# Attention probabilities of a query tile in one tile of up to 16 key tiles instead of two of 8, with a ring of five instead of ten

## The chip, the cores and the metric

One core of one Trainium2 chip runs the kernel. The metric is device time in microseconds (us). The engines named below are TensorE (PE; its weight loads are PEld), VectorE (DVE), ScalarE (ACT), GpSimd (POOL) and the DMA queue of SyncE (SP).

## What is computed

The reference is one layer of a decoder trunk on 2048 tokens of width 1024: a mixer of four groups and a gated feed-forward part. The change touches the two attention groups, FoX and NSA. Cut to what matters, per head and query row:

```
s = q @ k.T * scale + bias          # FoX: decay c_q - c_k, causal
p = softmax(where(mask, s, -1e30))  # NSA: table bias; masks of selected blocks / a window of 512
o = p @ v
```

FoX has 4 heads with all earlier keys. NSA has 4 heads with three branches: compressed keys, the selected blocks, and a sliding window. A query tile is 128 rows, so there are 16 query tiles. A query tile `qt` has up to `qt + 1` key tiles of 128 in FoX and in the selected branch, and at most 5 in the window branch.

## The kernel before

The attention stage works in units: one branch, one head and a pair `p` of query tiles (`q0 = 2p`, `a` = 0 or 1 for the tile of the pair). `fox_units` makes 4 x 8 units; `nsa_units` makes, per head, the pairs 0 to 3 of the selected branch and the pairs 0 to 7 of the window branch, and after all four heads the pairs 4 to 7 of the selected branch. The text calls these stretches FoX, early NSA (48 units) and late NSA (16 units). The blocks of the compressed branch (`add_cmp`) run beside FoX.

A unit goes through these steps (`add_unit`, lines as in the profile):

- score: two matmuls per group of up to 4 key tiles into an `S` bank of PSUM (L1045, L1046). `S` has two banks.
- bias: a DVE operation adds the bias to `S`, writes the sum into the tile `P` and keeps the row minimum in `mn` (L1060).
- expo: ACT takes the exponential of `P` in place and sums each row (L1082); an instruction that reads the sum out (ACTIVATION_READ_ACCUMULATOR) belongs to it. It runs only after the last bias of the row, since it needs the final minimum.
- turn: PE transposes two key tiles of both query tiles into a `tp` bank (L1118). Such a group of two key tiles is a slot.
- split: ACT, DVE and POOL make the high and low parts `ph` and `pl` of `tp` in one of three ways (L908, L911, L916, L920, L925). Way 0 is ACT and DVE, way 1 ACT, DVE and POOL, way 2 ACT twice and POOL.
- pv: PE multiplies both parts with the values into `obank` (L1140). At the end of a unit `obank` is copied by ACT (L962), transposed (L967), scaled into `t` on DVE (L975) or on ACT (L973), and added by POOL.

`P` is a tile of 128 x 1024, eight key tiles, and its ring holds `PBUFS = 10`. A row of more than eight key tiles takes two of them, `P[a][0]` and `P[a][1]`, has two expos and a `sums` operation on POOL (L1097) that adds the two row sums. A tile is taken by the bias that writes its first part and comes free with the last turn that reads it.

The order on all engines is written by a planner (`Plan.run`). Each operation has a key, and of those that can start at about the same time the smallest key is taken. The scores of a unit have the key of the slot 11 ahead of its first turn (`LEAD`), the expos of 2 ahead (`ELEAD`). The way of a split, and whether `t` is on ACT or on DVE, are chosen by the planner from what is queued on the two engines (`best`). On the chip each engine runs its own list in this order; an instruction that waits holds all behind it on its engine.

Of the kernel before, what the change touches and what calls it, by code (L numbers as in the profile page):

```python
# [12 lines left out]
F32 = mybir.dt.float32  # L13
# [24 lines left out]
R_FQ, R_FK, R_NQ, R_KC, R_KSW, R_POS = 46, 47, 48, 49, 50, 51  # L38
NROW = 83
LEAD = 11  # L40
PBUFS = 10
NPH = 6
NPF = 3
NS = 2
# [128 lines left out]
def kernel(ctx, tc, x, norm_mix, w_in, lru_conv_w, lru_conv_b, lru_w_gates, lru_b_gates,  # L173
# [4 lines left out]
    PE, ACT, DVE, POOL, SP = nc.tensor, nc.scalar, nc.vector, nc.gpsimd, nc.sync  # L178
# [16 lines left out]
    ident = const.tile([128, 128], F32, name="ident")  # L195
# [586 lines left out]
    with ExitStack() as B:  # L782
# [6 lines left out]
        pp = B.enter_context(tc.tile_pool(name="pp", bufs=PBUFS, reuse_waits="tile"))  # L789
# [15 lines left out]
        def buf(name):  # L805
            return Buf(rings[name])
# [192 lines left out]
        def add_unit(u, s0):  # L999
# [4 lines left out]
            c = {}  # L1004
            P, exps = [{}, {}], [{}, {}]
            order, pads, summed = [], [], []
            for a in range(2):
                qt = q0 + a
                w = qt + 1 - los[a]
                pad = -w % 4 if u["sel"] else 0  # L1010
                pads.append(pad)
                if u["near"] and w == 5:
                    parts = [(0, 3), (3, 2)]
                else:
                    cuts = sorted({0, w} | set(range(4 - pad, w, 4)))
                    parts = [(p, x - p) for p, x in zip(cuts, cuts[1:])]
                order += [(n, a, p, pw, w) for n, (p, pw) in enumerate(parts)]
                for x in range(0, w + pad, 8):
                    P[a][x // 8] = buf("P")
                if u["sel"] and qt >= 8:  # L1020
                    def both(a=a, qt=qt):
                        c["bt", a] = sm.tile([128, 512], F32, name="bt", tag="bt", bufs=3)
                        POOL.tensor_add(c["bt", a].rearrange("p (b k) -> p b k", k=64),
                                        win[:, h, 128:640].rearrange("p (b k) -> p b k", k=64),
                                        selm[:, qt - 8, 2 * qt - 6:2 * qt + 2, None].to_broadcast([128, 8, 64]))
                    bb = buf("bt")
                    prev["bt"] = [add("Pool", 1.23, lead - 1, both, take=[bb],
                                      after=[tabop, selop[qt]] + prev["bt"])]
                    summed.append((bb, prev["bt"][0]))
            lastT = [None, None]  # L1030
            for n, a, p, pw, w in sorted(order):
                pa = p + pads[a]
                qt, lo = q0 + a, los[a]
                b0 = lo + p
                m = 2 if pw == 1 else pw
                more = [(max(t0, b0), min(t1, b0 + pw), fn) for t0, t1, fn in u["extra"](qt)]
                more = [x for x in more if x[0] < x[1]]
                Sb = buf("S")

                def score(a=a, qt=qt, b0=b0, pw=pw, m=m, more=more, n=n):  # L1040
                    S = c["S", a, n] = pss.tile([128, 512], F32, name="S", tag="S")
                    qs = slice((qt % 4) * 128, (qt % 4) * 128 + 128)
                    ks = u["k"].tile[:, b0 * 128:(b0 + m) * 128]
                    dst = S[:, :m * 128]
                    PE.matmul(dst, u["q"].tile[:, 0, qs], ks, start=True, stop=False)  # L1045
                    PE.matmul(dst, u["q"].tile[:, 1, qs], ks, start=False, stop=True)  # L1046
                    for t0, t1, fn in more:
                        PE.matmul(S[:, (t0 - b0) * 128:(t1 - b0) * 128], identr, fn(t0, t1), start=False, stop=True,
                                  skip_group_check=True)

                opens = n == 0 or pa % 8 == 0
                selects = u["sel"] and qt >= 8 and p + pw == w

                def bias(a=a, qt=qt, b0=b0, pw=pw, pa=pa, n=n, opens=opens, selects=selects):
                    if n == 0:
                        c["mn", a] = sm.tile([128, 4], F32, name="mn", tag="mn")
                    if opens:
                        c["P", a, pa // 8] = pp.tile([128, 1024], F32, name="P", tag="P")
                    x0, mn = pa % 8 * 128, c["mn", a]
                    DVE.tensor_tensor_reduce(c["P", a, pa // 8][:, x0:x0 + pw * 128], c["S", a, n][:, :pw * 128],  # L1060
                                             c["bt", a] if selects else u["bias"](qt, b0, b0 + pw), 1.0,
                                             mn[:, n - 1:n] if n else big, OP.add, OP.min, mn[:, n:n + 1])
                S = add("PE", 0.107 * (max(m, 2) + len(more)), lead + n * 0.01, score, take=[Sb],
                        use=[u["k"].buf, u["q"].buf],
                        after=[u["k"].op, u["q"].op] + prev["S"])
                prev["S"] = [S]
                Pb = P[a][pa // 8]
                cb, cops = u["biases"](qt, b0)
                if selects:
                    cb, cops = [summed[a][0]], [summed[a][1]]  # L1070
                lastT[a] = add("DVE", dve_time(pw * 128), lead + n * 0.01, bias, take=[Pb] if opens else [],
                               use=[Sb] + cb + ([] if opens else [Pb]),
                               after=[S] + cops + ([lastT[a]] if n else []))
                if p + pw == w:
                    for x in P[a]:
                        c0, c1 = pads[a] * 128 if x == 0 else 0, min(8, w + pads[a] - 8 * x) * 128

                        def expo(a=a, x=x, c0=c0, c1=c1, n=n):
                            if "sum" not in c:
                                c["sum"] = sm.tile([128, 2, 2], F32, name="sum", tag="sum")  # L1080
                            t = c["P", a, x][:, c0:c1]
                            ACT.activation(t, t, AF.Exp, bias=c["mn", a][:, n:n + 1], scale=-1.0,  # L1082
                                           accum_out=c["sum"][:, x, a:a + 1])
                        exps[a][x] = add("Activation", exp_time(c1 - c0), s0 - ELEAD + 0.1 * x, expo, use=[P[a][x]],
                                         after=[lastT[a]])
# [23 lines left out]
            for gi, g in enumerate(groups):  # L1109
# [5 lines left out]
                def turn(cells=cells, tp=tp):  # L1115
                    tp["tp"] = pst.tile([128, 2, 256], F32, name="tp", tag="tp")
                    for si, a, kt in cells:
                        PE.transpose(tp["tp"][:, si, a * 128:(a + 1) * 128],  # L1118
                                     c["P", a, kt // 8][:, kt % 8 * 128:(kt % 8 + 1) * 128], ident)
                used = sorted({(a, kt // 8) for _, a, kt in cells})  # L1120
                runs = []
                for si, sl in enumerate(g):
                    if sl[0] == sl[1]:
# [446 lines left out]
    with ExitStack() as Dx:  # L1570
# [156 lines left out]
        x = dict(x0)  # L1727
# [211 lines left out]
```

## Time and profile before

| | |
|---|---|
| median of 3 runs | 2710.84 us (2707.81 to 2711.39) |
| the profiled execution | 2708.36 us, of which span 2706.6 us |
| PE busy over the span | 2618.8 us (97%) |
| attention stage, 590 to 1196 us of the span | 606 us |

The stage lies in three stretches: FoX from 590 to about 850 us, early NSA to about 1040 us and late NSA to 1196 us. Feed-forward work follows it and needs its results, so idle time of PE in the stage is time of the whole. "Busy" counts an engine's instructions as the profiler shows them; the ends of matmuls are modelled.

### The profile page before, as it was taken

Reading aid. Unit: us, or ns where it says so; the run is one execution under the profiler, and the core shown is the slowest. Engines: PE = TensorE matmul, PEld = TensorE weight load, DVE = VectorE, ACT = ScalarE, POOL = GpSimd, SP = SyncE. Lnnn points to the kernel's source line nnn. Section 1 sums busy time; section 2 is a strip of 40 time slices with the busy share of each in tenths; the row PEclk is TensorE's granted clock in tenths of the full one; section 3 lists DMA queues with packets and bytes.
Section 4 is the critical chain, followed back from the end, with each engine's and each line's share of the span. In section 5 each row is a group of like instructions: output and inputs, shape, how many; then the busy total and the mean of one; then the engine's idle time right before and its main releaser. Section 6 shows DMA issues by size and latency. Waiting matters only on the chain.

```text
span 2706.6 us, 39620 instructions
## 1 busy us (share of the span) xinstructions
PE 2618.8 (97%) x13483; PEld 2207.1 (82%) x13483; DVE 1720.9 (64%) x3757; ACT 1339.4 (49%) x2916; POOL 976.2 (36%) x1103
## 2 busy tenths in 40 slices
PE   7999988999988999999999999999999999999999
PEld 5799767888987998888877888887888888888887
DVE  5763487347899889877777566667666555333333
ACT  5432475149988898885544333334233324333331
POOL 1101124214576577750234433433441123224440
PEclk9999999999999999999999999999999999999999
DMA  5444313264332211047855544455543235664653
GB/s 167 118 113 117 119 59 131 76 176 112 101 88 62 65 48 40 24 157 229 256 191 164 186 137 159 157 163 155 176 158 107 79 112 183 215 192 127 185 183 101
DMA packets 314808, 364.73 MB, mean 135 GB/s; under 512 B 25503, under 2 KB 214126, under 8 KB 313838
## 3 DMA queue, kind: packets, MB, share of 16 engines
q1 hardware_dynamic: 312430, 358.02, 42.5%
q10 hardware_dynamic: 2176, 4.19, 0.4%
q8 instruction: 106, 1.74, 0.3%
q14 instruction: 96, 0.79, 0.1%
HBM read 240.24 MB, written 121.90 MB: 134 GB/s over the span
## 4 chain that ended last, share of the span: by engine, by line
PE 77%; DVE 9%; issue 6%; DMA 3%; ACT 3%; POOL 2%; SPq 0%; POOLq 0%; DVEq 0%; ACTq 0%
PE gu L1758 9%; PE gu L1757 9%; PE gu L1756 9%; PE d L1885 5%; PE d L1887 5%; PE d L1886 5%; PE obank L1140 5%; PE tp L1118 4%; PE z L216 4%; PE z L217 4%; PE z L215 4%; PE S L1045 3%; PE S L1046 2%; PE px L215 2%; PE px L217 2%
## 5 line engine op out<-in xcount | busy, mean ns | idle before, releaser
L1756 PE MATMUL gu<-xh,g 128*128 128x512 f32 x1232 | 487.6, 396 | 7.6 <-DVE gq L1718 4.8
L1757 PE MATMUL gu<-xh,g 128*128 128x512 f32 x1232 | 487.0, 395 | 2.1 <-POOL g L1543 2.1
L1758 PE MATMUL gu<-xl,g 128*128 128x512 f32 x1232 | 486.7, 395 | 1.7 <-DVE xl L1666 1.7
L1543 POOL TENSOR_TENSOR g<-guraw,g 128x512 fp32r<-128x512 f32 x136 | 185.6, 1385 | 520.8 <-ACT g L1542 510.4
L1816 DVE TENSOR_TENSOR a<-araw,a 128x512 fp32r<-128x512 f32 x150 | 117.1, 783 | 268.9 <-ACT a L1815 268.9
L1756 PEld LDWEIGHTS gu<-xh,g 128*128 128x128 f32 x1232 | 232.4, 189 | 63.2 <-issue 5.6
L1757 PEld LDWEIGHTS gu<-xh,g 128*128 128x128 f32 x1232 | 232.4, 189 | 56.8 <-POOL g L1543 3.1
L1758 PEld LDWEIGHTS gu<-xl,g 128*128 128x128 f32 x1232 | 232.3, 189 | 56.7 <-DVE xl L1666 2.6
L925 POOL TENSOR_TENSOR pl<-pf,ph 128x512 fp32r<-128x512 f32 x174 | 224.0, 1294 | 109.1 <-ACT ph L911 47.8
L1082 ACT ACTIVATE P<-P,mn 128x1024 f32<-128x1024 f32 (+7 forms) x256 | 226.4, 892 | 17.7 <-DVE mn L1060 17.3
L1815 ACT CAST a<-araw 128x512 fp32r<-128x512 f32 x150 | 93.2, 622 | 279.2 <-PE d L1887 262.7
L1885 PE MATMUL d<-b,a 128*128 128x512 f32 x584 | 231.0, 396 | 0.0
L1886 PE MATMUL d<-b,a 128*128 128x512 f32 x584 | 231.0, 396 | 0.0
L1887 PE MATMUL d<-b,a 128*128 128x512 f32 x584 | 231.0, 396 | 0.0
L1140 PE MATMUL obank<-ph,v 128*128 128x256 f32 (+1 forms) x744 | 198.6, 294 | 3.7 <-ACT ob L962 3.6
L1118 PE MATMUL tp<-ident,P 128*128 128x128 f32 x1368 | 199.5, 273 | 2.0 <-DVE t L975 0.9
L1045 PE MATMUL S<-k,q 128*128 128x512 f32 (+2 forms) x432 | 175.5, 409 | 15.8 <-DVE mn L1060 11.0
L1140 PE MATMUL obank<-pl,v 128*128 128x256 f32 (+1 forms) x744 | 185.3, 283 | 3.4 <-POOL pl L925 1.9
L1118 PEld LDWEIGHTS tp<-ident,P 128*128 128x128 f32 x1368 | 160.1, 141 | 15.3 <-DVE t L975 1.2
L1827 POOL TENSOR_TENSOR b<-braw,b 128x512 fp32r<-128x512 f32 x73 | 101.9, 1409 | 182.7 <-ACT b L1826 181.2
L1046 PE MATMUL S<-k,q 128*128 128x512 f32 (+2 forms) x432 | 152.6, 355 | 0.0
L1542 ACT CAST g<-guraw 128x512 fp32r<-128x512 f32 x228 | 130.0, 618 | 42.5 <-DVE guraw L1613 34.9
(512 smaller groups left out, 6256.3 us busy)
## 6 DMA issues: line engine op xcount, KB each, us to landing
guraw<-in_w_gate_up_dram SPq DMA_DIRECT2D x88, 512.0 KB
araw<-hf_d SPq DMA_DIRECT2D x150, 256.0 KB
hf_d<-uq SPq DMA_DIRECT2D x88, 256.0 KB
q<-qk_d SPq DMA_DIRECT2D x80, 256.0 KB
hf_d<-gq SPq DMA_DIRECT2D x66, 256.0 KB
xt<-in_x_dram SPq DMA_DIRECT2D x32, 512.0 KB
xraw<-xf_d SPq DMA_DIRECT2D x24, 512.0 KB
dnraw<-in_w_down_dram SPq DMA_DIRECT2D x44, 256.0 KB
```

The lines of the kernel that those rows point to most:

```text
L925: POOL.tensor_sub(tp["pl"], tp["pf"], f(tp["ph"]))
L1045: PE.matmul(dst, u["q"].tile[:, 0, qs], ks, start=True, stop=False)
L1046: PE.matmul(dst, u["q"].tile[:, 1, qs], ks, start=False, stop=True)
L1082: ACT.activation(t, t, AF.Exp, bias=c["mn", a][:, n:n + 1], scale=-1.0, accum_out=c["sum"][:, x, a:a + 1])
L1118: PE.transpose(tp["tp"][:, si, a * 128:(a + 1) * 128], c["P", a, kt // 8][:, kt % 8 * 128:(kt % 8 + 1) * 128], ident)
L1140: PE.matmul(c["o"][:, cs], u["v"].tile[:, kt, :], tp[x][:, si, cs], start=gi == 0 and i == 0, stop=last and i == len(todo) - 1, skip_group ...
L1756: PE.matmul(p, wh[:, k], xh[:, k], start=j < 4 and k == 0, stop=False, skip_group_check=True)
L1757: PE.matmul(p, wl[:, k], xh[:, k], start=False, stop=False, skip_group_check=True)
L1758: PE.matmul(p, wh[:, k], xl[:, k], start=False, stop=k == HK - 1, skip_group_check=True)
L1885: PE.matmul(p, a[0][:, ts], w[0], start=first, stop=False, skip_group_check=True)
L1886: PE.matmul(p, a[0][:, ts], w[1], start=False, stop=False, skip_group_check=True)
L1887: PE.matmul(p, a[1][:, ts], w[0], start=False, stop=stop_, skip_group_check=True)
```

## The change

`PBUFS` goes from 10 to 5 and a new constant `WIDTH = 16` takes the place of every 8 in the division of a row into tiles. `P` becomes 128 x 2048, so that every row has one tile, one expo and no `sums`. The ring takes the same 40 KiB of each partition. A row of 8 key tiles or less, which took one of ten tiles, takes one of five.

```diff
-PBUFS = 10
+PBUFS = 5
+WIDTH = 16
...
-                for x in range(0, w + pad, 8):
-                    P[a][x // 8] = buf("P")
+                for x in range(0, w + pad, WIDTH):
+                    P[a][x // WIDTH] = buf("P")
...
-                opens = n == 0 or pa % 8 == 0
+                opens = n == 0 or pa % WIDTH == 0
...
-                        c["P", a, pa // 8] = pp.tile([128, 1024], F32, name="P", tag="P")
-                    x0, mn = pa % 8 * 128, c["mn", a]
+                        c["P", a, pa // WIDTH] = pp.tile([128, WIDTH * 128], F32, name="P", tag="P")
+                    x0, mn = pa % WIDTH * 128, c["mn", a]
...
-                        c0, c1 = pads[a] * 128 if x == 0 else 0, min(8, w + pads[a] - 8 * x) * 128
+                        c0, c1 = pads[a] * 128 if x == 0 else 0, min(WIDTH, w + pads[a] - WIDTH * x) * 128
...
-                                     c["P", a, kt // 8][:, kt % 8 * 128:(kt % 8 + 1) * 128], ident)
-                used = sorted({(a, kt // 8) for _, a, kt in cells})
+                                     c["P", a, kt // WIDTH][:, kt % WIDTH * 128:(kt % WIDTH + 1) * 128], ident)
+                used = sorted({(a, kt // WIDTH) for _, a, kt in cells})
```

The planner writes a new order on all engines. One line is added ahead, so a line of the changed kernel has a number one higher.

ACT in early NSA, at the window branch of head 2, pair 5. Before, the two exponentials are the first row, and the last row copies the unit's first slot:

```order
L1082 ACTIVATE P,sum<-P,mn 128x640 x2
L908 COPY pf<-tp 128x512
L1082 ACTIVATE P,sum<-P,mn 128x640
L962 COPY ob<-obank 128x256
L908 COPY pf<-tp 128x512
L911 CAST ph<-tp 128x512
L908 CAST ph<-tp 128x256
L908 CAST ph<-tp 128x512
L908 COPY pf<-tp 128x512
L1082 ACTIVATE P,sum<-P,mn 128x640
L908 CAST ph<-tp 128x256
L908 COPY pf<-tp 128x512
```

Now the two exponentials are the first and the third row, and the last row casts the unit's first slots:

```order
L1083 ACTIVATE P,sum<-P,mn 128x640
L974 ACTIVATE t<-fp,r 128x128 x2
L1083 ACTIVATE P,sum<-P,mn 128x640
L909 COPY pf<-tp 128x512
L909 CAST ph<-tp 128x512
L1083 ACTIVATE P,sum<-P,mn 128x640
L963 COPY ob<-obank 128x256
L909 CAST ph<-tp 128x256
L909 CAST ph<-tp 128x512 x2
```

Between the unit's second exponential and the first use of its transposed tile lie 5 instructions instead of 10.

ACT in late NSA, at the selected branch of head 1, pair 7, with rows of 15 and 16 key tiles. Before, each row has two exponentials, and the last row here casts the first slot:

```order
L1082 ACTIVATE P,sum<-P,mn 128x896
L908 COPY pf<-tp 128x512
L911 CAST ph<-tp 128x512
L908 CAST ph<-tp 128x512 x3
L1082 ACTIVATE P,sum<-P,mn 128x1024
L908 COPY pf<-tp 128x512
L911 CAST ph<-tp 128x512
L1082 ACTIVATE P,sum<-P,mn 128x1024 x2
L908 CAST ph<-tp 128x256
L908 CAST ph<-tp 128x128
L908 CAST ph<-tp 128x512
```

Now each row has one, and the copy of the first slot is the last but one row:

```order
L1083 ACTIVATE P,sum<-P,mn 128x1920
L1083 ACTIVATE P,sum<-P,mn 128x2048
L909 CAST ph<-tp 128x512
L909 CAST ph<-tp 128x256
L909 CAST ph<-tp 128x128
L1083 ACTIVATE P,sum<-P,mn 128x1152
L909 COPY pf<-tp 128x512
L912 CAST ph<-tp 128x512
```

Four exponentials of the unit became two.

Counted over the whole order: 192 exponentials of `P` instead of 256, no `sums` instead of 64; of the 128 scalings into `t`, 56 pairs of instructions on ACT instead of 33 and one instruction each on DVE for the rest; way 2 takes 73 slots instead of 85, way 1 takes 98 instead of 89, and whole slots of way 0 are 121 instead of 118. In early NSA alone `t` is on ACT 28 times instead of 12 and way 2 falls from 21 to 14; in FoX `t` is on ACT 14 times instead of 7. PE has the same instructions as before in another order.

## Rows read from the trace of the kernel before

**Rows 1.** The page: busy time, share of the span and instructions of each engine.
```profile
PE 2618.8 (97%) x13483; PEld 2207.1 (82%) x13483; DVE 1720.9 (64%) x3757; ACT 1339.4 (49%) x2916; POOL 976.2 (36%) x1103
```
**Rows 2.** Busy time by stretch; columns as its first line says, in us.
```profile
core 0: us, PE busy (x) PEld busy (x) DVE busy (x) ACT busy (x) POOL busy (x), PEclk, DMA share, GB/s
590.00:850.00 260.00, 244.31 (x1803) 223.69 (x1803) 225.88 (x776) 229.47 (x617) 139.32 (x212) 0.99 0.38 101
850.00:1040.00 190.00, 182.36 (x1403) 170.84 (x1402) 167.70 (x604) 172.42 (x469) 129.17 (x215) 0.99 0.23 62
1040.00:1196.00 156.00, 152.83 (x1116) 137.59 (x1115) 131.17 (x353) 135.48 (x302) 117.51 (x166) 1.00 0.14 45
```
**Rows 3.** Waits of PE, 750 to 900 us: us in total, times, longest.
```profile
PE S L1045 <- DVE mn L1060: 8.3, 8, 2.7
PE Sc L1244 <- DVE cmn L1251: 3.2, 2, 2.9
```
**Rows 4.** Waits of DVE, 850 to 1040 us: us in total, times, longest.
```profile
DVE P L1060 <- PE S L1046: 5.1, 12, 1.2
DVE P L1060 <- PE tp L1118: 2.5, 3, 1.5
```
**Rows 5.** Groups by shape on ACT, DVE and POOL, 586 to 1202 us: busy, mean ns.
```profile
L973 ACT ACTIVATE t<-fp,r 128x128 f32<-128x128 f32 x44 | 14.0, 376 | 3.8 <-PE fp L967 3.7
L920 DVE TENSOR_TENSOR pl<-tp,ph 128x512 fp32r<-128x512 f32 x118 | 79.1, 683 | 11.2 <-ACT ph L908 8.9 <-PE fp L967 2.1
L916 DVE CAST ph<-pf 128x512 fp32r<-128x512 f32 x89 | 57.1, 643 | 5.9 <-ACT pf L908 5.8
L975 DVE TENSOR_TENSOR t<-fp,r 128x256 f32<-128x256 f32 x74 | 31.0, 419 | 16.4 <-PE fp L967 14.1 <-issue 1.5 <-POOL r L1092 0.3
L1097 POOL TENSOR_TENSOR sum<-sum 128x1 f32<-128x1 f32 x64 | 11.2, 195 | 12.5 <-ACT P L1082 12.5
```
**Rows 6.** Timeline of ACT, stretch of the first place above: start, us, instruction.
```profile
985.56 0.86 ACT L1082 ACTIVATE P<-P,mn 128x640 f32<-128x640 f32 x1
...
986.39 0.84 ACT L1082 ACTIVATE P<-P,mn 128x640 f32<-128x640 f32 x1
987.11 0.21 ACT L1082 ACTIVATION_READ_ACCUMULATOR P<-P,mn 128x1 f32 x1
987.20 0.59 ACT L908 COPY pf<-tp 128x512 f32<-128x512 f32 x1
...
989.33 0.59 ACT L908 COPY pf<-tp 128x512 f32<-128x512 f32 x1
989.81 0.60 ACT L911 CAST ph<-tp 128x512 fp32r<-128x512 f32 x1
```
**Rows 7.** Timeline of PE: the first turn of the same unit.
```profile
991.83 0.82 PE L1118 MATMUL tp<-ident,P 128*128 128x128 f32 x6
```
**Rows 8.** Timeline of ACT, the second place above (late NSA).
```profile
1113.96 1.17 ACT L1082 ACTIVATE P<-P,mn 128x1024 f32<-128x1024 f32 x1
...
1115.11 1.15 ACT L1082 ACTIVATE P<-P,mn 128x1024 f32<-128x1024 f32 x1
...
1116.24 1.03 ACT L908 CAST ph<-tp 128x256 fp32r<-128x256 f32 x3
```
**Rows 9.** Timeline of PE: the first turn of the unit of rows 8.
```profile
1113.48 0.60 PE L1118 MATMUL tp<-ident,P 128*128 128x128 f32 x4
```
**Rows 10.** Timeline of DVE: first bias of the window unit of head 1, pair 7.
```profile
946.65 0.61 DVE L1060 CUSTOM_DVE_ANT_0 P<-S,win,big 128x384 f32<-128x384 f32 x1
```
**Rows 11.** Timeline of ACT: the last exponential of the unit of rows 10.
```profile
950.54 0.87 ACT L1082 ACTIVATE P<-P,mn 128x640 f32<-128x640 f32 x1
951.28 0.22 ACT L1082 ACTIVATION_READ_ACCUMULATOR P<-P,mn 128x1 f32 x1
```
**Rows 12.** Timeline of PE: first and last turn of the unit of rows 10.
```profile
958.43 0.82 PE L1118 MATMUL tp<-ident,P 128*128 128x128 f32 x6
...
960.70 0.38 PE L1118 MATMUL tp<-ident,P 128*128 128x128 f32 x2
```

More of the change, by code (lines that the diff above doesn't have):

```diff
@@ L1057, in bias @@
                     if opens:
-                        c["P", a, pa // 8] = pp.tile([128, 1024], F32, name="P", tag="P")
-                    x0, mn = pa % 8 * 128, c["mn", a]
-                    DVE.tensor_tensor_reduce(c["P", a, pa // 8][:, x0:x0 + pw * 128], c["S", a, n][:, :pw * 128],
+                        c["P", a, pa // WIDTH] = pp.tile([128, WIDTH * 128], F32, name="P", tag="P")
+                    x0, mn = pa % WIDTH * 128, c["mn", a]
+                    DVE.tensor_tensor_reduce(c["P", a, pa // WIDTH][:, x0:x0 + pw * 128], c["S", a, n][:, :pw * 128],
                                              c["bt", a] if selects else u["bias"](qt, b0, b0 + pw), 1.0,
@@ L1066, in add_unit @@
                 prev["S"] = [S]
-                Pb = P[a][pa // 8]
+                Pb = P[a][pa // WIDTH]
                 cb, cops = u["biases"](qt, b0)
```

## The prediction

> **What bounds the kernel now.** I read the page first, to see which engine fills the span. PE is busy for 2618.8 us of it, 97% [rows 1]. The change lies in the attention stage alone, so I then read the busy times of its three stretches. The reader is to see how near the other engines come to PE there. In FoX PE is busy for 244.3 of 260 us, in early NSA for 182.4 of 190, in late NSA for 152.8 of 156 [rows 2]. So PE is idle for 15.7 + 7.6 + 3.2 = 26.5 us in 606. That is all a better supply of PE can give back here, since its own instructions stay the same. ACT has 229, 172 and 135 us, DVE 226, 168 and 131: in early NSA that is 91% and 88%, little less than PE's 96%. Third, the waits. Between 750 and 900 us PE waits above all with a score, for the bias that frees its bank, 8.3 us [rows 3]. DVE's bias in early NSA waits for a score 5.1 us, and for the turn that frees a tile only 2.5 us in 3 times [rows 4]. The ring of P limits little today. Last I followed single tiles on the timelines, to see how long a tile is held and for what; this is the part on which the change acts.
>
> **Exponentials.** Of 256 there remain 192; 64 go, 32 in FoX and 32 in late NSA, where rows have more than eight key tiles. Early NSA has no such row. An exponential of 640 columns takes 0.83 us from its start to the next instruction's first time and 0.81 the second [rows 6], one of 1024 takes 1.13 [rows 8]. That is (1.13 - 0.82) / 384 = 0.81 ns a column and 0.30 us fixed, with the reading of the sum in it. The elements stay, the fixed part goes: 64 x 0.30 = 19 us of ACT. PE does not wait for ACT in any large amount, so this lies beside PE's work and is worth nothing by itself.
>
> [...]
>
> **What the planner does with that.** The order has 23 more scalings into t on ACT, as two instructions of 376 ns, and 12 fewer second casts of way 2, of 0.48 us from start to start (989.33 to 989.81) [rows 5, 6]. ACT: -19 + 23 x 0.75 - 12 x 0.48 = -7.5 us in all. But in early NSA, which saves no exponential, it is 16 x 0.75 - 7 x 0.48 = +8.6 us, from 172 to 181 us of 190, or 95%. DVE: -23 x 0.419 + 9 x 0.643 (casts of way 1) + 3 x 0.683 (way 0) = -1.8 us [rows 5]. POOL loses 64 sums of 195 ns, 12.5 us, and three subtractions; nothing critical waits for them.
>
> **The ring.** A row of eight key tiles or less held one of ten tiles and now holds one of five. Take a window unit of early NSA. Its first bias starts at 946.65 [rows 10], its last exponential is read out at 951.50 [rows 11], its first turn starts at about 958.65 (the third of the six matmuls of the piece at 958.43), and its last ends at 961.08 [rows 12]. So its tile is held for 14.4 us, and for 7.1 of these it only lies ready. The work itself is 14.4 - 7.1 = 7.3 us. Early NSA has 48 units in 190 us [rows 2], one in 3.96 us, with two tiles each. Ten tiles are five units, 19.8 us; five tiles are 2.5 units, 9.9 us. At the same pace a tile may therefore lie ready for 9.9 - 7.3 = 2.6 us instead of 7.1. The order says the same: at its first place 5 instead of 10 ACT instructions lie between the exponential and the first use of its transposed tile, and those 10 were 987.2 to about 992.05, 4.9 us [rows 6, 7], so 5 are some 2.4 us.
>
> Is a cushion of 2.5 us enough? Late NSA is the nearest row: the unit of its head 1, pair 7 starts its first turn at 1113.48 [rows 9], while two of its four exponentials start only at 1113.96 and 1115.11 [rows 8]. It runs without any cushion, and PE is idle there for 2% only [rows 2]. That is why I take little. Lower bound: 0. Upper bound: the ring is never full. Today 14.4 of 19.8 us are used, 73%. If five tiles are used no better and 1 us of cushion is needed, the pace is (7.3 + 1.0) / (0.73 x 2.5) = 4.55 us, or 48 x 0.59 = +28 us. I take +5, near the lower end, for ACT at 95% and the cushion cut to a third.
>
> **Long rows.** A first turn now needs two whole exponentials, 2 x (0.30 + 2048 x 0.00081) = 3.9 us, where two first halves did, 2 x 1.13 = 2.3 us. It can start 1.6 us later in each of 32 units. What hides it is the other unit's work that the order puts between: at the second place four ACT instructions. I take 0; without that cover it would be 32 x 1.6 = 51 us. A long tile also comes free only after its last turn, where the first half came free in the middle of the unit. The number of rows in flight stays 2.5 units, so I take +1 for FoX, whose short rows at the start of a head (pairs 0 to 3) also have half the tiles; if their cushion is not enough, it is bounded by the same 28 us scaled to their 16 units of 48, +9.
>
> **Relief.** In FoX between 750 and 900 us PE waits for the bias, that is for DVE. FoX has 7 scalings fewer on DVE, 2.9 us: I take -2, between 0 and -2.9. In late NSA PE is idle for 3.2 us: I take -1, between 0 and -3.2.
>
> **Sum.** +5 + 1 - 2 - 1 = +3 us on the profiled execution's 2708.4, 2711.4. The median of the runs lies 2.5 us above that execution, so 2714 us, 0.1% above 2710.8. What a measurement can tell from no change is about 0.2%, 5.4 us.
>
> **Rivals.** *The ring becomes the bound of early NSA* (slower). The place is the bias that opens a tile on DVE. It waits for PE's last turn two and a half units back; behind it in DVE's list stand the subtractions and casts of the splits and the scaling of t, and for these PE's pv waits, which is ahead of the next turns. It decides from the point at which work and cushion of a tile exceed 9.9 us, with 7.3 of work from the rows. Halfway to the upper bound it costs +14: 2725 us. Against it: 2.6 us are left. For it: three engines at 88 to 96%, and a list that cannot step aside. [...]
>
> *The relief of ACT reaches PE* (faster). ACT loses 19 us of fixed cost in FoX and late NSA, where PE is idle for 15.7 + 3.2 = 18.9 us [rows 2]. If half of that idle time goes, it is -9.4 and, with +1 for the ring, -8: 2703 us. Against it: PE's waits are for DVE's bias [rows 3], and DVE's work falls by 1.8 us only.
>
> *The relief is taken back*: the planner spends what the exponentials save on scalings, so that only the order changes. That is within my forecast, at 0: 2711 us.
>
> **Chances.** Forecast, within 0.2% of 2710.8 (the third rival in it): 0.42, from 2706 to 2716. The ring as the bound: 0.35, mostly 2717 to 2728, with a tail to 2739 and above. Relief reaching PE: 0.23, 2701 to 2705. The range leaves out a tenth at either end: 2702 to 2728. So faster 0.23, same 0.42, slower 0.35.
>
> **What would show it.** In the changed trace, early NSA: ACT at some 95%, PE's idle time at 10 to 15 us of that stretch instead of 7.6, and waits of DVE's bias for the turn well over 2.5 us. If those waits pass 15 us and the stretch is longer than 200 us, the ring is the bound. If the stretch from 590 to 850 gets 5 us shorter, the relief reached PE. Late NSA should keep its length within 2 us; if it grows by more, the cover of the long exponentials is gone. I am wrong altogether if the time moves outside the stage.

## The result: 1.2% slower, and the profile after

| | before | after |
|---|---|---|
| median of 4 runs each | 2709.57 us (2707.81 to 2711.39) | 2742.95 us (2740.54 to 2745.55) |
| the profiled execution | 2708.36 us | 2740.54 us |
| its span | 2706.6 us | 2738.7 us |

The ratio is 1.0118, with a 95% interval from 1.0101 to 1.0136. That is +33 us. The forecast of 2714 us is missed, and so is the range up to 2728 us. It went to the side of the first rival, slower, and past the 2725 us of that one too.

The page of the kernel after, first its busy times and then two groups of its list; a group has its busy time, the mean of one, and the idle time of the engine ahead of it with what ended that:

```profile
PE 2637.1 (96%) x13483; PEld 2215.8 (81%) x13483; DVE 1733.9 (63%) x3746; ACT 1328.2 (48%) x2822; POOL 963.7 (35%) x1036
...
L1083 ACT ACTIVATE P<-P,mn 128x640 f32<-128x640 f32 (+5 forms) x192 | 206.7, 1079 | 33.0 <-DVE mn L1061 31.7
...
L1046 PE MATMUL S<-k,q 128*128 128x512 f32 (+2 forms) x432 | 175.1, 408 | 26.5 <-DVE mn L1061 26.0
```

The same two groups on the page of the kernel before:

```profile
L1082 ACT ACTIVATE P<-P,mn 128x1024 f32<-128x1024 f32 (+7 forms) x256 | 226.4, 892 | 17.7 <-DVE mn L1060 17.3
...
L1045 PE MATMUL S<-k,q 128*128 128x512 f32 (+2 forms) x432 | 175.5, 409 | 15.8 <-DVE mn L1060 11.0
```

The exponentials of `P` fell by 226.4 - 206.7 = 19.7 us, as worked out ahead (19). Everything else got worse. ACT now waits for the bias (`mn` is written by it) 31.7 us instead of 17.3, and PE waits for it 26.0 us instead of 11.0.

PE's busy time grew by 18 us [rows 1], although its instructions are the same 13483. The granted clock tells part of why. Busy times by stretch, in the columns of [rows 2]; the stretches are head 3 of FoX, early NSA, late NSA, and 12 us behind the stage. After:

```profile
796.00:880.00 84.00, 68.79 (x468) 61.05 (x468) 74.64 (x249) 61.17 (x162) 48.94 (x77) 0.94 0.22 57
880.00:1072.00 192.00, 181.50 (x1339) 165.21 (x1339) 161.87 (x561) 164.68 (x453) 110.47 (x192) 0.97 0.20 56
1072.00:1224.00 152.00, 147.54 (x1065) 132.44 (x1063) 126.23 (x341) 123.78 (x231) 108.79 (x129) 1.00 0.14 46
1224.00:1236.00 12.00, 9.89 (x43) 8.39 (x44) 4.61 (x17) 6.26 (x22) 4.48 (x5) 0.72 0.94 343
```

The same work before:

```profile
795.00:868.00 73.00, 64.09 (x455) 57.01 (x454) 67.32 (x243) 61.40 (x174) 47.74 (x81) 0.98 0.27 68
868.00:1050.00 182.00, 175.84 (x1351) 164.99 (x1350) 161.08 (x567) 163.62 (x436) 124.78 (x204) 0.99 0.20 56
1050.00:1200.00 150.00, 145.64 (x1063) 131.07 (x1062) 123.79 (x330) 128.31 (x286) 112.15 (x156) 1.00 0.15 50
```

The clock column falls from 0.98 to 0.94 at the end of FoX, from 0.99 to 0.97 in early NSA, and to 0.72 in the 12 us right behind the stage. Single stretches show 0.50, as one is shown further down.

The table goes from the first turn of the stage (591.0 us before, 587.9 after) and cuts it at the last turn of each part. "Idle" is the time without an instruction of PE in the timeline. "Clock" is an estimate of what half speed cost: half of the time in which the granted clock was at 0.50 and PE was not idle, since from one matmul of 256 columns to the next it took 0.22 us there and 0.12 at 1.00 (shown further down). Microseconds, before and after:

| part | length | PE idle | clock | matmuls into `S` |
|---|---|---|---|---|
| FoX, heads 0 to 2 | 203.8, 207.6 | 8.3, 12.5 | 1.4, 1.7 | 311, 290 |
| FoX, head 3 | 73.6, 84.3 | 8.9, 15.2 | 1.7, 4.2 | 81, 92 |
| early NSA | 181.3, 191.9 | 6.2, 10.5 | 1.7, 3.7 | 324, 321 |
| late NSA | 146.9, 151.8 | 3.2, 4.1 | 0.0, 0.0 | 200, 213 |
| sum | 605.6, 635.6 | 26.6, 42.3 | 4.8, 9.6 | 916, 916 |

The stage starts 3.1 us earlier and is 30.0 us longer, so it ends 27 us later. Of the 30.0, 15.7 are idle time of PE and 4.8 are its half clock; 9.5 show as neither. Most of these may be waits too: the end of a matmul is modelled, so a short wait behind it can be hidden in it. Counted from one matmul's start to the next at full clock, what goes more than 0.1 us beyond the median step of its kind adds up to 45.2 us in 136 places before and 69.1 us in 203 after. That is an estimate from the two traces. It grew by 23.9 us, where the idle time at full clock grew by 11.7. Another 5 us come behind the stage, 4.0 of them from more time at half clock.

The waits say what PE lacked. PE's weight loads show it most fully: in the kernel after they wait 40.7 us for the bias, where the matmuls wait 26.0. Waits of PEld from 584 to 1230 us, before and then after (us in total, times, longest):

```profile
PEld S L1045 <- DVE mn L1060: 19.8, 33, 3.0
```
```profile
PEld S L1046 <- DVE mn L1061: 40.7, 53, 5.0
```

A score finds its bank of `S` not yet read by the bias. That wait alone grew by 20.9 us. In early NSA alone (868 to 1050 us before, 880 to 1072 after):

```profile
PEld S L1045 <- DVE mn L1060: 5.7, 8, 2.8
```
```profile
PEld S L1046 <- DVE mn L1061: 12.9, 21, 3.2
```

The wait that the prediction had watched, the bias for the turn that frees a tile, stays small. Waits of DVE in the kernel after, from 880 to 1072 us (early NSA):

```profile
DVE P L1061 <- PE tp L1119: 7.7, 9, 1.5
```

So 7.7 us, against 2.5 in [rows 4]; no wait is over 1.5 us. (The stretch of [rows 4] still has the end of FoX in it. By its turns early NSA lies from 868 to 1050 us before, where these waits are 1.0 us.)

**One hole, row by row.** From the end of head 2 of FoX to the start of early NSA (773 to 896 us), DVE also chooses the key blocks of the selected branch: for each of the eight query tiles 8 to 15 one uninterrupted run of 15 small instructions (`select`), a selection. The planner books it as one operation of 2.5 us. Timeline of DVE in the kernel after (start, us, instruction):

```profile
812.38 0.43 DVE L1332 TENSOR_TENSOR sa<-ps__8206 128x32 f32<-128x32 f32 x1
812.84 1.25 DVE L1333 TENSOR_TENSOR sa<-sa,ps__8206 128x32 f32<-128x32 f32 x1
814.00 1.31 DVE L1334 TENSOR_TENSOR sb<-ps__8206 128x32 f32<-128x32 f32 x1
815.35 0.93 DVE L1335 TENSOR_SCALAR sb<-sb 128x32 f32<-128x32 f32 x1
816.32 0.19 DVE L1336 SCALAR_TENSOR_TENSOR sa<-sa,sb 128x32 f32<-128x32 f32 x1
...
818.15 0.18 DVE L1346 TENSOR_SCALAR selm<-sa 128x32 f32<-128x32 f32 x1
818.24 0.74 DVE L1061 CUSTOM_DVE_ANT_0 P<-S,crow,mn 128x512 f32<-128x512 f32 x1
```

Timeline of PE there (in brackets the idle time ahead of a row and what ended it):

```profile
814.23 0.28 PE L1141 MATMUL obank<-ph,v 128*128 128x256 f32 x1
814.35 0.28 PE L1141 MATMUL obank<-pl,v 128*128 128x256 f32 x1
819.05 0.58 PE L1046 MATMUL S<-k,q 128*128 128x256 f32 x1 [4.42 <-DVE mn L1061]
...
820.71 0.41 PE L1141 MATMUL obank<-ph,v 128*128 128x256 f32 x1
820.93 0.41 PE L1141 MATMUL obank<-pl,v 128*128 128x256 f32 x1
```

And the windows of 4 us around it, in the columns of [rows 2]:

```profile
812.00:816.00 4.00, 2.63 (x20) 2.29 (x20) 3.93 (x6) 2.65 (x7) 4.00 (x4) 1.00 0.00 0
816.00:820.00 4.00, 0.95 (x4) 0.95 (x5) 3.47 (x19) 0.70 (x1) 0.24 (x1) 0.71 0.00 0
820.00:824.00 4.00, 4.00 (x20) 4.00 (x20) 2.64 (x13) 2.95 (x8) 0.00 (x0) 0.50 0.00 0
```

The selection holds DVE from 812.38 to 818.33. No bias runs in that time. One more score fills the bank that the last bias had read (812.76); from then on both banks of `S` are full and no new score starts. PE lives on that and on the tiles that lie ready, 2.25 us long, then stands still for 4.42 us until the next bias. The clock falls within this hole and is 0.50 behind it. In the window of 820 to 824 PE is busy without a gap, but from one matmul of 256 columns to the next it takes 0.22 us (820.71 to 820.93) where it took 0.12 (814.23 to 814.35). The comparable selection of the kernel before lasts 5.5 us, from 806.44 to 811.92. PE has work for 3.5 us of it and stands still for 2.54:

```profile
809.67 0.28 PE L1140 MATMUL obank<-pl,v 128*128 128x256 f32 x1
812.49 0.47 PE L1045 MATMUL S<-k,q 128*128 128x512 f32 x1 [2.54 <-DVE cmn L1251]
```

Over all eight selections DVE spends 31.2 us before and 33.9 after. The PE idle time that falls into them and the 1 us behind each is 12.9 us before and 19.3 after (9.3 and 15.0 without that 1 us).

**The cushion of a tile.** The unit of [rows 10 to 12] in the kernel after, on DVE, ACT and PE:

```profile
972.34 0.61 DVE L1061 CUSTOM_DVE_ANT_0 P<-S,win,big 128x384 f32<-128x384 f32 x1
```
```profile
977.27 0.21 ACT L1083 ACTIVATION_READ_ACCUMULATOR P<-P,mn 128x1 f32 x1
```
```profile
977.53 0.82 PE L1119 MATMUL tp<-ident,P 128*128 128x128 f32 x6
...
980.64 0.73 PE L1119 MATMUL tp<-ident,P 128*128 128x128 f32 x5
```

Its tile is taken at 972.3, read out at 977.5, first transposed at 977.75 (the third of the six matmuls of the piece) and free at about 981. It is held for 8.7 us instead of 14.4, and lies ready for 0.3 us instead of 7.1. FoX is no different: from the last exponential that a unit's first turn needs to that turn it is 7.1 us on the mean of its 32 units before, and 2.7 after.

### The profile page after: what moved, and what is told of

Same layout as the page of the kernel before. It is cut to its first block, busy times and chain, and to the rows that moved or that the text cites. A ratio compares the mean times of both kernels' runs of the same rounds, so it can differ in the third digit from the quotient of the medians.

```text
span 2738.7 us, 39488 instructions
## 1 busy us (share of the span) xinstructions
PE 2637.1 (96%) x13483; PEld 2215.8 (81%) x13483; DVE 1733.9 (63%) x3746; ACT 1328.2 (48%) x2822; POOL 963.7 (35%) x1036
## 4 chain that ended last, share of the span: by engine, by line
PE 80%; DVE 9%; issue 4%; ACT 3%; POOL 2%; DMA 2%; SPq 0%; POOLq 0%; DVEq 0%; ACTq 0%
PE gu L1758 9%; PE gu L1759 9%; PE gu L1757 9%; PE d L1888 5%; PE d L1887 5%; PE d L1886 5%; PE obank L1141 5%; PE z L217 5%; PE z L218 5%; PE z L216 5%; PE tp L1119 3%; PE S L1046 2%; PE px L216 2%; PE px L218 2%; PE px L217 2%
## 5 line engine op out<-in xcount | busy, mean ns | idle before, releaser
L926 POOL TENSOR_TENSOR pl<-pf,ph 128x512 fp32r<-128x512 f32 x171 | 220.9, 1298 | 122.3 <-ACT ph L912 58.1
L1083 ACT ACTIVATE P<-P,mn 128x640 f32<-128x640 f32 (+5 forms) x192 | 206.7, 1079 | 33.0 <-DVE mn L1061 31.7
L1119 PE MATMUL tp<-ident,P 128*128 128x128 f32 x1368 | 191.7, 274 | 1.7 <-DVE pl L921 0.9
L1141 PEld LDWEIGHTS obank<-pl,v 128*128 128x128 f32 x744 | 142.9, 192 | 19.1 <-POOL pl L926 10.1
```

The lines of the kernel that those rows point to most:

```text
L926: POOL.tensor_sub(tp["pl"], tp["pf"], f(tp["ph"]))
L1119: PE.transpose(tp["tp"][:, si, a * 128:(a + 1) * 128], c["P", a, kt // WIDTH][:, kt % WIDTH * 128:(kt % WIDTH + 1) * 128], ident)
L1141: PE.matmul(c["o"][:, cs], u["v"].tile[:, kt, :], tp[x][:, si, cs], start=gi == 0 and i == 0, stop=last and i == len(todo) - 1, skip_group ...
```

## The experiments

Five explanations compete; the letters are those of the texts that were written ahead of the runs. **The ring** (A): short rows have half the places, so scores can run only half as far ahead. **The merge** (B): one long exponential where two halves had let a first turn start early. **The order** (C): the planner writes another order after any edit, and the old one may have been a lucky one. **The selections** (D): DVE's long blocks drain PE where the cushion is small. **The booking** (E): the planner counts too little time for a selection. Every ratio is to the kernel before, measured in the same series, with its 95% interval. Where a text speaks of LEAD, that is how many slots ahead the scores are put.

### Ring against merge

**share_l10.** The wide tiles of the changed kernel, but a unit with short rows puts both rows into one tile, the second from column 1024 on. Short rows then have ten places again. LEAD is 10, without which this order doesn't come about.

```diff
-LEAD = 11
+LEAD = 10
...
-                    P[a][x // WIDTH] = buf("P")
+                    P[a][x // WIDTH] = P[0][0] if pair and a else buf("P")
```

> Wide tiles, ring of five, merged exponentials, but a unit whose rows have at most eight key tiles puts both of its rows into one wide tile (second row from column 1024). So short units are again five deep as before the change, long units stay at 2.5. LEAD is 10 instead of 11. Theory A (the halved ring for short rows costs the time): 2712 us, between 2704 and 2720. Theory B (the merged exponential and the late release of a long tile cost it): 2740, above 2733. Theory C (luck of the planner's order): anywhere from 2705 to 2745, and the run with LEAD 10 alone moves as much.

Measured: 2728.37 us, 1.0061 (1.0043 to 1.0079). About half of the loss comes back.

**split.** The changed kernel with the exponential of a long row in two halves again, and the sums that belong to them; the tile stays one.

```diff
-                    for x in P[a]:
-                        c0, c1 = pads[a] * 128 if x == 0 else 0, min(WIDTH, w + pads[a] - WIDTH * x) * 128
+                    for x in range(1 + (w + pads[a] > 8)):
+                        c0, c1 = pads[a] * 128 if x == 0 else 1024, min(8 * x + 8, w + pads[a]) * 128
```

> Wide tiles and a ring of five as in the change, but the exponential of a row above eight key tiles is done in two halves with two sums, as before the change. Theory A (ring): the merge was worth nothing and its undoing costs nothing on PE, 2743 us, between 2737 and 2752. Theory B (merge delays the first turn of long rows): at least half of the loss comes back, 2710 to 2727. Theory C (luck of the order): anywhere in between.

Measured: 2737.41 us, 1.0098 (1.0077 to 1.0118). The interval overlaps that of the changed kernel. The merge is at most a small part, and 64 exponentials more cost PE nothing.

**w8_p8.** The kernel before with eight narrow tiles (`PBUFS = 8`): no wide tile, no long exponential.

> The kernel before with eight tiles of eight key tiles in the ring instead of ten, nothing merged: 4 short units in flight instead of 5, 2 long ones instead of 2.5. Theory A (ring): a part of the loss without any wide tile, 2713 to 2728. Theory B (merge): 2710, within 4 us of before. Theory C (luck of the order): either.

Measured: 2726.44 us, 1.0055 (1.0040 to 1.0070). A smaller ring costs by itself: PE's weight loads wait 27.3 us for the bias here instead of 19.8.

**after_l10.** The changed kernel with LEAD 10, to stand beside share_l10.

> The changed kernel with LEAD 10 instead of 11, which gives the planner another order with the same tiles. Theory A and B: 2743 us within 6, since neither the ring nor the merge changes. Theory C (luck of the order): it moves by more than 10 us, to below 2733 or above 2753.

Measured: 2745.43 us, 1.0126 (1.0111 to 1.0142). LEAD alone doesn't help the changed kernel.

### The order by itself

**before_l10.** The kernel before with LEAD 10 and nothing else.

> The kernel before with LEAD 10 instead of 11: same tiles, same ring of ten, another order. It is the control for the run with shared wide tiles, which had LEAD 10 and stood 17 us above before. Theory A (ring): 2711 us within 5, as LEAD moved the changed kernel by 2.5 us only. Theory C (the order of before is a lucky one among its neighbours, and any other loses): 2718 to 2730.

Measured: 2720.62 us, 1.0033 (1.0020 to 1.0045). A neighbouring order costs 0.33%, 9 us, with all ten tiles.

**w8_p9.** Nine narrow tiles.

> The kernel before with nine tiles of eight key tiles instead of ten. Eight cost 15 us. Theory A (ring, the loss grows as tiles go): 2713 to 2721, between ten and eight. Theory C (luck of the order): as slow as eight or slower, above 2724, or as fast as ten, below 2712.

Measured: 2723.64 us, 1.0044 (1.0025 to 1.0062). Nearly as slow as eight. A loss in proportion to the ring would have been smaller, which suggests that part of it comes from leaving the order of before.

**share_split_l10.** share_l10 with split exponentials: the order of a full ring, wide tiles only as storage.

> Shared wide tiles (short units put both rows into one) with LEAD 10, and the exponentials of long rows in two halves with two sums again. It differs from before in the grain of the tiles alone: a long row's first half isn't freed early, a short unit's rows are taken and freed together. If the merged exponential is what is left of the loss: 2711 within 5. If the grain of the tiles is: 2728 within 6, as with merged exponentials.

Measured: 2724.79 us, 1.0054 (1.0038 to 1.0070).

At LEAD 10 this gives a ladder in which each step changes one thing, and with it the order, in per cent of the kernel before (27.1 us each): +0.33 for the order (before_l10), +0.21 for tiles given out and freed as wide ones (share_split_l10), +0.07 for the merge (share_l10), +0.65 for the half ring of short rows (after_l10). Together they are 1.26%. The intervals are some 0.15% to either side, so the second and the third step can hardly be told from nothing. The last is the largest and the only one far outside: 17.6 us. The waits agree. PE's weight loads wait for the bias of `S` for 23.8 us in before_l10, 20.4 in share_l10 and 41.1 in after_l10 (584 to 1240 us), as for 19.8 and 40.7 in the kernels before and after.

**share_nsa.** Sharing in NSA only, LEAD 11; FoX keeps the half ring.

> The changed kernel (LEAD 11) with shared wide tiles in the two NSA stretches only; FoX as changed. Theory A (each stretch pays for its own ring): FoX as in the changed kernel, 292 us from first to last turn, early NSA shorter than 191.9 by some 5 us as in the run with sharing everywhere, in all 2737 us within 5. If early NSA lost because FoX came late or cold, it stays at 190 or more and the whole at 2743.

Measured: 2738.32 us, 1.0100 (1.0085 to 1.0115). Early NSA takes 186.2 us instead of 191.9, and FoX stays at 293.2, as after the change (292.0). So sharing in NSA gives back 5.7 of the 10.6 us of early NSA and nothing of FoX's.

### The selections

**nosel_before** and **nosel_after.** Both kernels with the body of `select` replaced, in the same order of operations. The choice of blocks is left out: every block counts as selected.

```diff
-            v = [ps[:, i:i + 125:4] for i in range(5)]
...
-            DVE.tensor_scalar(selm[:, qt - 8], a, -2e38, BIG, op0=OP.is_gt, op1=OP.mult)
+            DVE.memset(selm[:, qt - 8], BIG)
```

> The kernel before, in the same order, but each of the eight block selections (L1331 to L1345, some 17 DVE instructions, 31 us of DVE in all) is left out and one memset marks every block as selected; the planner still counts 2.5 us for it. Theory D (PE runs dry in a selection, since the bias stands behind it on DVE, and TensorE's clock falls after it): 12.9 us of PE's idle time lie in selections, so 2697, between 2688 and 2702. Theory A alone (the ring, no special place): at most 5 us faster, above 2705.

> The same in the changed kernel. 19.3 us of PE's idle time lie in selections there, and stretches at half clock follow them. Theory D: 2716, between 2708 and 2722; and the distance to the run of before without selections is 22 us or less instead of 33. Theory A alone: 2735 or more, and the distance stays at 30 or above.

Measured: 2701.39 us, 0.9971 (0.9958 to 0.9984), and 2723.03 us, 1.0049 (1.0031 to 1.0068). FoX takes 273.0 and 273.6 us: the 14.6 us that the change costs there are gone. These are one trace each, and that of nosel_before shows an execution of 2707.2 us, 5.8 above its median. The distance between the two kernels falls from 33 to 21.6 us by the medians, and from 32.2 to 15.1 by the profiled executions, so 12 to 17 us of the loss go with the selections. Early NSA still differs by 9.2 us (181.9 and 191.1), late NSA by 5.1. Waits of PE's weight loads, 584 to 1230 us, nosel_before and then nosel_after:

```profile
PEld S L1045 <- DVE mn L1060: 13.2, 28, 1.2
```
```profile
PEld S L1046 <- DVE mn L1061: 25.8, 49, 1.8
```

The longest wait falls from 3.0 and 5.0 us to 1.2 and 1.8: the large holes were the selections'. What stays are 21 more short waits.

**chop_before** and **chop_after.** The planner gets a selection as four operations and can put biases between them.

```diff
+                for part, time in enumerate((1.2, 1.2, 0.9, 0.7)):
+                    prevop = add("DVE", time, s + 16 + 2 * a,
```

> The kernel before with each selection given to the planner as four operations of 1.2, 1.2, 0.9 and 0.7 us instead of one of 2.5, so that a bias can go between them; nothing is left out. Theory D: PE's holes in selections shrink, 2702 within 5, a kernel faster than before. Theory C (the order of before is a lucky one, any other loses): 2715 to 2725.

> The same in the changed kernel: selections as four operations. Theory D: at least 8 us come back, 2728 to 2735. Theory A alone: 2743 within 6.

Measured: 2715.04 us, 1.0017 (1.0005 to 1.0030), and 2743.07 us, 1.0123 (1.0106 to 1.0140). A miss: nothing is gained. In chop_after the selections, from first to last part, are spread over 46.3 us in all, and PE is still idle for 14 us in them and right behind.

**seltime_before** and **seltime_after.** The planner is told 4.2 us for a selection, about the measured mean (33.9 / 8), instead of 2.5.

> The kernel before with the planner told 4.2 us for a selection instead of 2.5 (the trace shows 2.9 to 5.5); nothing is left out. Theory E (the planner books too little time, so it lays too little work beside a selection): 2700 to 2707, faster than before. Theory C (any other order than that of before loses): 2713 to 2724.

> The same in the changed kernel: 4.2 us for a selection. Theory E: 2725 to 2736, with FoX at 285 or less. If half the depth leaves nothing to lay beside a selection, whatever it is booked at: 2743 within 6, FoX 290 or more.

Measured: 2724.77 us, 1.0042 (1.0028 to 1.0056), and 2743.11 us, 1.0111 (1.0094 to 1.0127). The wrong booking is not the cause either: with a right one FoX is 295.1 us long.

**nosel_share_l10.** share_l10 without the choice of blocks (every block counts as selected).

> Shared wide tiles with LEAD 10 and the selections left out (one memset each, same order). With them it takes 2728, and 18.5 us of PE's idle time lie in selections. Theory D: FoX falls from 287 to 273 within 2 as in both other kernels, early NSA stays at 186, 2711 in all, between 2705 and 2716. If the selection's holes are only half of FoX's excess: FoX 280, 2718 or more.

Measured: 2708.84 us, 0.9987 (0.9977 to 0.9997). FoX takes 266.5 us, less than the 273 of either kernel without selections. With ten places and no long block on DVE, 16.8 us (0.62%) of nosel_after's time are gone (LEAD is 10 here and 11 there).

**poolsel_before** and **poolsel_after.** The same order; the three additions that open a selection run on POOL, behind its last gathering of the scores.

```diff
+                            POOL.tensor_add(sa, v[1], v[2])
+                            POOL.tensor_add(sa, sa, v[3])
+                            POOL.tensor_add(sb, v[0], v[4])
...
-            DVE.tensor_add(a, v[1], v[2])
-            DVE.tensor_add(a, a, v[3])
-            DVE.tensor_add(b, v[0], v[4])
```

> The kernel before in the same order, but the three additions at the head of each selection (L1331 to L1333, both inputs in SBUF) are issued on POOL right behind the last gather instead of on DVE; nothing is left out. On DVE some of them take 1.2 to 1.3 us where the same form takes 0.2 beside them. Theory D: selections on DVE fall from 31 us in all to about 20, PE's idle time in them from 12.9 to about 6, 2703, between 2697 and 2708. If POOL is late with them and DVE waits as long for it: 2711 within 5.

> The same in the changed kernel. Theory D: idle time in selections falls from 19.3 to about 9 us and less half clock follows, 2731, between 2724 and 2736. If POOL is late with them: 2743 within 6.

Measured: 2712.00 us, 0.9999 (0.9989 to 1.0008), and 2734.98 us, 1.0078 (1.0063 to 1.0094). The additions are cheap there, on the timeline of POOL in poolsel_after:

```profile
805.47 0.25 POOL L1323 TENSOR_TENSOR sa<-ps__8206 128x32 f32<-128x32 f32 x1
805.79 0.27 POOL L1324 TENSOR_TENSOR sa<-sa,ps__8206 128x32 f32<-128x32 f32 x1
806.02 0.27 POOL L1325 TENSOR_TENSOR sb<-ps__8206 128x32 f32<-128x32 f32 x1
```

In the kernel after, the idle time of PE in the selections and the 1 us behind each falls from 19.3 to 14.8 us and the whole by 0.4%, 11 us. In the kernel before, the same edit takes 4.2 us off the selections (31.2 to 27.0) and moves the time by nothing. Here a shorter block on DVE is worth something only in the kernel with the small cushion.

### Depth without wide tiles, in early NSA

**waste_nsa.** The kernel before, ten narrow tiles in memory, but the planner books two places for a short row of NSA. The order there is that of five places, while no instruction can wait for memory that isn't there.

```diff
+            W = [[buf("P")] if not u["new"] and q0 + 2 - min(los) <= 8 else [] for _ in range(2)]
...
-                lastT[a] = add("DVE", dve_time(pw * 128), lead + n * 0.01, bias, take=[Pb] if opens else [],
+                lastT[a] = add("DVE", dve_time(pw * 128), lead + n * 0.01, bias, take=[Pb] + W[a] if opens else [],
```

> The kernel before with its ten tiles of eight key tiles and two exponentials in long rows, but in both NSA stretches the planner books two places of the ring for a row of at most eight key tiles, though it uses one tile. So the order of early NSA is that of a half as deep ring, while on the chip ten tiles are there. Theory A (the depth in the order makes the loss of early NSA): from first to last turn early NSA takes 188 to 193 us instead of 181.3, FoX stays at 277 within 4, late NSA at 147 within 2, 2720 in all, between 2715 and 2726. Theory B (the wide tile itself, or waiting on the chip for a free tile): early NSA 180 to 185, 2711 to 2715.

Measured: 2715.31 us, 1.0007 (0.9998 to 1.0017). Early NSA takes 190.2 us, 8.9 more than before, as in the changed kernel (+10.6). Five more matmuls into `S` lie in it (329), some 1.2 us of that. Steps of PE that go more than 0.1 us beyond their median, counted as above, add up to 16.4 us there, against 10.6 before and 17.0 after. FoX and late NSA are 2.2 and 2.6 us shorter than before, which no run explains, so the whole hardly moves. The longer early NSA thus comes from how far ahead the order lets scores run, not from the wide tile and not from a wait for it.

## Why the prediction was wrong

**FoX, +1 - 2: the step that failed.** The measured term is +14.6. The prediction bounded FoX's short rows by early NSA's upper bound scaled down, +9, and asked only whether a tile comes free in time. It didn't ask for how long another job on the engine that supplies PE can hold the supply up. The selections were in the trace of before: eight of them on DVE, 2.9 to 5.5 us each, with PE idle for 12.9 us in and right behind them. What lay ready bridged the rest of each, and that cushion was cut from 7.1 to 2.7 us. Without selections the FoX of the two kernels differs by 0.6 us instead of 14.6 (one trace each), and share_nsa shows that the ring of NSA has no part in it. The ring isn't all of it, though. With LEAD 10 FoX takes 284.9 us with ten narrow tiles (before_l10), 287.0 with shared places (share_l10) and 293.4 with five (after_l10). So another order costs 7.5 us there by itself, and five places 6.4 more. The idle time in and right behind the selections is 17.2, 18.5 and 18.7 us in these three: with that order, what five places cost does not show in the selections, and where in FoX it lies is open. The relief of -2 can't be seen beside this.

**Early NSA, +5: right mechanism, too small.** It is +10.6: 4.3 of idle time, 2.0 of half clock, 4.3 that show as neither. The cushion of 2.6 us at the old pace was worked out rightly from its rows. By its turns early NSA lasted 181.3 us and not 190, which makes it 2.1; in the unit shown it came out as 0.3. The inference from it failed. Late NSA runs without a cushion and loses only 2%, but its long rows may give DVE and PE more even work; it was no witness for short rows. waste_nsa gives the stretch nearly this length (+8.9) without a wide tile, though the whole kernel moved by 0.1% only. Of the signs named, PE's idle time did come, 10.5 us. The 7.7 us of waits of a bias for its turn are below the 15 that were to mean "ring bound". The place named for the rival, the bias that waits for the turn, is not where the time goes. It shows one step on, at the score that waits for the bias: 12.9 us in early NSA instead of 5.7 (waits of PE's weight loads). ACT at 95% was wrong too; it is 164.68 of 192, 86%.

**Late NSA, -1.** It is +4.9. Part of that is moved work: 13 more of the stage's 916 matmuls into `S` lie in it, since scores run less far ahead of the boundary. One of 512 columns takes 0.23 us from start to start, on PE's timeline in the kernel after:

```profile
1121.52 0.39 PE L1046 MATMUL S<-k,q 128*128 128x512 f32 x1
1121.75 0.40 PE L1047 MATMUL S<-k,q 128*128 128x512 f32 x1
```

So they are up to 3.0 us, and the idle time grew by 0.9. Late NSA takes 148 to 154 us in the runs with 213 or 214 of these matmuls in it (after, split, after_l10, nosel_after, seltime_after, poolsel_after) and 144 to 151 in all others, which have 198 to 206. The prediction named the cover of the long exponentials as the suspect. Split, which has 213 and no long exponential, takes 148.1, so they cost 3.7 us there at most; the two causes aren't told apart further.

**Half clock: not in the sum at all.** The stretches read ahead showed 0.99 or more [rows 2], so the clock stood in no term. It is 4.8 us in the stage and 4.0 behind it, a quarter of the whole. "Wrong altogether if the time moves outside the stage" was half true: 27 us are inside, 5 outside.

**Right.** The exponentials gave 19.7 us of ACT (19 worked out), and PE got nothing of it: the second rival, relief reaching PE, is refuted. Long rows' later first turn is worth nothing that these intervals can show (split, and the ladder's 0.07%). The first rival was right in sign, and its price of 14 for early NSA is not far from 10.6; it left out FoX. The trace agrees on its cause, too few places, with share_l10 and waste_nsa beside it, though the gaps of PE run from short waits to 4.8 us and end with a bias, not with a tile that comes free.

**What stays open.** The order of before is better by some 9 us than that of LEAD 10, and nine tiles cost 12; why this order is good isn't settled, and with it how much of the 33 us is the loss of a lucky order. chop shows that the blocks' length is not cured by offering the planner gaps; why PE is still idle for 14 us then was not traced. 9.5 us of the stage show neither as idle time nor as clock; that they are short waits is an estimate. No version here beats the kernel before: the best that keep the wide tile and compute everything are share_split_l10 and share_l10, at 1.0054 and 1.0061.

## What to carry to other kernels

Size a ring not only by its mean pace but by the longest other job on each engine that feeds it: the work that lies ready must last as long as that job does (in the hole shown above 2.25 us of work stood against a selection of 5.95). In these runs that alone was not enough: in before_l10 the tiles of FoX lie ready for 7.3 us on the mean, as before the change, and PE still stands for 17.2 us in and right behind the selections. Read the cushion off as the time from "ready" to "first use", and set it against the longest block in the list of the feeding engine, in every stage apart. When large and small rows share a ring, a tile made for the large ones takes depth from the small ones, and an engine that is not on the path gains time that nobody collects (19.7 us of exponentials on ACT here).

## What the runs showed of the hardware

**The clock fell in or behind several holes of PE.** PE stood still for 4.4 us, from 814.63 to 819.05. The granted clock was 0.71 on the mean of 816 to 820 and then 0.50, while PE was busy without a gap. The same came with the hole of 4.8 us at 851, which has 0.67 on the mean of the 4 us from 856 on. Another fall came behind a shorter hole, of 1.63 us at 891: the clock was at 0.50 from 892.8 to 903, and the longer hole of 2.9 us at 894 lies within that time. Timeline of PE in the kernel after:

```profile
855.72 0.79 PE L1046 MATMUL S<-k,q 128*128 128x512 f32 x1 [4.78 <-DVE mn L1061]
...
892.65 0.49 PE L1046 MATMUL S<-k,q 128*128 128x256 f32 x1 [1.63 <-DVE mn L1061]
...
896.86 0.69 PE L1046 MATMUL S<-k,q 128*128 128x384 f32 x1 [2.87 <-DVE mn L1061]
```

Windows around the last two, in the columns of [rows 2]:

```profile
888.00:892.80 4.80, 3.17 (x25) 2.92 (x24) 4.39 (x24) 4.35 (x12) 1.68 (x2) 1.00 0.28 72
892.80:893.90 1.10, 1.10 (x4) 0.76 (x4) 1.07 (x4) 0.00 (x0) 0.89 (x1) 0.50 1.07 341
...
896.80:903.00 6.20, 6.14 (x24) 5.60 (x25) 4.58 (x20) 2.45 (x7) 1.92 (x6) 0.50 0.30 89
903.00:907.00 4.00, 3.89 (x33) 3.44 (x33) 1.46 (x4) 3.65 (x12) 1.76 (x6) 1.00 0.00 0
```

So these holes cost more than their length: behind the first, the clock stayed at 0.50 until 824.5, with PE busy from 819.05 on. Before, the hole of 2.54 us at 809.95 already had 0.68 behind it (812 to 816). It did not come with every hole: the one of 2.71 us that ended at 845.98 before has 1.00 on the mean of 845 to 855.

**Small DVE instructions stretched beside POOL.** In the selection above two of the additions took 1.25 and 1.31 us, and one scaling 0.93; POOL was busy for the whole of 812 to 816, until 815.24 with subtractions of 1.3 us each (the mean of L926 on the page is 1298 ns) and then with an addition. Others of the same 128 x 32 took 0.19. So it was in all eight selections, before and after: the additions and scalings that took over 0.3 us ran beside a busy POOL, and those that ran while POOL stood still took 0.18 to 0.22. The trace of poolsel_after, listed by tile (duration in ns, min/median/max), has both in one row, and none of it for the maxima:

```profile
L1339 DVE TENSOR_TENSOR sa<-sa,sf x8: 191/377/1215, 773.2 to 888.0; 128x32 f32<-128x32 f32 x8
...
L1343 DVE MAX8 m<-sa x8: 195/195/196, 773.9 to 888.5; 128x8 f32<-128x32 f32 x8
```

So 0.19 becomes up to 1.3 us, longer by no more than one subtraction of POOL. The stretched ones aren't only those with two inputs, since the scaling has one. What makes them longer was not shown beyond this. It is part of why a selection took 2.9 us once and 6.4 another time (at 862.05 and 848.64 in the kernel after).
